# Narrow fp32 products cut into pieces of 64 columns, step sizes as four-strip products, a carried state read by halves of its rows

## The chip, the cores and the metric

The program runs on one core of one Trainium2 chip. What counts is the device time of one execution in microseconds (us). A core has TensorE (PE, matrix products, with PEld for its weight loads), VectorE (DVE), ScalarE (ACT), GpSimd (POOL), SyncE (SP, which here issues every transfer) and 16 DMA engines. TensorE's clock has two levels, 2.4 and 1.2 GHz; the profile gives the granted share.

## The reference, cut to what matters

One inference step of a hybrid decoder: 16 meta tokens and 1024 prompt tokens, and 8 sequences that decode one token each. There are 2 layers, D = 1024, and three groups of heads run side by side in a layer.

```python
for l in range(2):
    h = rmsnorm(x)
    q, k, v, u, z, xBC, dt = split(h @ W_in)      # dt: 4 columns, one for each SSD head
    A = rmsnorm(sliding_window_attention(q, k, v))   # 8 heads, window 128, sinks
    B = rmsnorm(glu(gelu(s5_scan(u))))               # diagonal state space
    # SSD: xs, B, C from a causal convolution of xBC; step = softplus(dt + bias)
    # chunks of 128 tokens: y = (C B^T * decay) (step * xs) + C (carried state) * decay + D * xs
    C = rmsnorm(ssd(xs, B, C, step) * silu(z))
    x = x + concat(A, B, C) @ W_out
    x = x + swiglu(rmsnorm(x))
y = rmsnorm(x)
```

## The kernel before, in words

Features lie on the partitions, tokens along the free dimension. The 1048 tokens are cut into two halves (528 and 520 columns), each half into two chunks (264 and 264, or 264 and 256; in the last layer's output stages 256 and 256). The unit of program is (layer, half).

The large projections are done by `mm3` (lines 206 to 213): weights and activations are split into a rounded part and a rest, and each tile of 128 x 128 weights makes three float32r products with 264 or 256 moving columns. I call these the wide products: L211, L212 and L213, 16,896 instructions of TensorE's 20,006. Among them the code weaves the small products of the mixers, which are plain fp32. An fp32 product shows in the trace as two MATMUL records, each with its weight load; a float32r product, a bf16 product and a transpose (against `ident`, L614, L971, L1252 and others) show as one.

The lines that the change touches:

- `rstd_diag` (239): the sum of squares over the partitions, as products of pieces of `acc` against a column of ones, one moving column each (L245). A chunk of 264 gives three products with 88 weight columns, one of 256 two with 128, a block of attention one with 128. Its result goes through ACT, DVE, another product (L258, or L1171 in attention) to the engine that scales by it.
- `in_proj` (321) with `weights_dt` (189): one of its 15 steps computes `dt`, 16 products for each chunk against a tile that is 4 columns wide in substance and padded to 128 (L339, L340); the sum is scaled on DVE and stored as 4 rows.
- `s5_prep` (371): taps of the S5 convolution, 128 weight columns against 32 moving ones, two products summed (L624).
- `ssd` (841): reads `dt`, turns it to tokens on partitions (L899, L904), sums the decays with `tri` and `ones` (L929, L943), then for each chunk of 128 tokens the products L1016 (inside the chunk), L1019 (with the state `hT` carried into the chunk) and L1024 (the new state). For L1019 the C matrix was padded with zeros to 128 rows in two copies `Cz`, one for each group:

```python
V.tensor_mul(cz4[:, 1], cz4[:, 0], Cz[1][:, cols].unsqueeze(1).to_broadcast([128, 2, nq]))
V.tensor_mul(cz4[:, 0], cz4[:, 0], Cz[0][:, cols].unsqueeze(1).to_broadcast([128, 2, nq]))
```

- `attn_dec` (1305): the decode step's scores and values, 128 weight columns of a cache against 8 moving ones for each of 8 sequences (L1326, L1361).

The order on every engine is set when the program is built, by a scheduler that follows an estimated timeline and priorities; on the chip TensorE then takes its products in that order. Accumulators are six banks `x` (`pmx`, three for the tag `o`, three for `a`) and two banks `b` (`pbig`).

Of the kernel before, what the change touches and what calls it, by code (L numbers as in the profile page):

```python
# [31 lines left out]
EPS = 1e-6  # L32
MT = 'u0 u1 k v q0 q1 q2 q3 xs0 xs1 B C dt z0 z1'.split()


def build(ctx, tc, A):
# [87 lines left out]
    evn = [0]  # L124

    def evac(out, in_):
        evn[0] += 1
        if evn[0] % 2:
            S.copy(out, in_)
        else:  # L130
            V.tensor_copy(out, in_)
# [56 lines left out]

    def weights_dt(l, mi):

        raw = wp.tile([128, 8, 128], F32, tag="wr", name=nm("wr"), bufs=2)
        with tc.high_priority(offset=3000):
            load(raw, A["w_in"][l, mi])
        wh = wp.tile([128, 8, 128], F32R, tag="wh", name=nm("wh"))
        S.copy(wh, raw)
        wl = wp.tile([128, 8, 128], F32R, tag="wl", name=nm("wl"))
        S.copy(wl, raw)
        V.tensor_sub(wl[:, :, 32:36], raw[:, :, 0:4], wh[:, :, 0:4].bitcast(F32))
        return wh, wl

    def split(dst, cols, src, eng=None):
# [37 lines left out]
    def rstd_diag(acc, n, scale):  # L239

        nb = -(-n // 128)
        w = n // nb
        ps = pmx()
        for j in range(nb):
            PE.matmul(ps[0:w, 504 + j:505 + j], acc[:, j * w:j * w + w], ones[:, 0:1], start=True, stop=True)  # L245
        sm = small()[0:w, 0:nb]
        S.activation(sm, ps[0:w, 504:504 + nb], AF.Sqrt, bias=epst[0:w, 0:1], scale=scale)
        V.reciprocal(sm, sm)
        dg = ftp.tile([128, 264], F32, tag="dg", name=nm("dg"))
        V.tensor_mul(dg[0:w, :n].rearrange("p (j q) -> p j q", j=nb), ident[0:w, 0:w].unsqueeze(1).to_broadcast([w, nb, w]),  # L250
                     sm.unsqueeze(2).to_broadcast([w, nb, w]))
        return w, dg
# [38 lines left out]
    for l in range(DEPTH):  # L291
        for hf in range(2):
            T = TH[hf]
            for n_ in ("xs0", "xs1", "B", "C", "k", "v", "z0", "z1"):
                P[l, hf, n_] = dram([128, T], n_)
            P[l, hf, "dt"] = dram([4, T], "dt")
            P[l, hf, "u"] = dram([2, 128, 8 * NK8[hf]], "u")
# [8 lines left out]
    def in_norm(l, hf, new):  # L306
# [4 lines left out]
        for c0, c1 in CH[hf]:  # L311
            acc = None
            for k, t in enumerate(x[hf]):
# [3 lines left out]
                acc = add_square(acc, t[:, c0:c1], c1 - c0)  # L317
            rstd_sum(acc, c1 - c0, 1.0 / D, rs[:, c0:c1])
        return xn, rs

    def in_proj(l, hf, xr, early=0):
# [5 lines left out]
        for mi, name in enumerate(MT):  # L327
            w = weights(A["w_in"][l, mi], 8) if name != "dt" else weights_dt(l, mi)
            st = stp.tile([128, 528], F32, tag="st", name=nm("st"))
            for c0, c1 in CH[hf]:  # L330
# [4 lines left out]
                else:  # L335
                    ps = pbig()
                if name == "dt":
                    for k in range(8):
                        PE.matmul(ps[:, :n], w[1][:, k, :], xn[k][:, 0, c0:c1], start=(k == 0), stop=False)  # L339
                        PE.matmul(ps[:, :n], w[0][:, k, :], xn[k][:, 1, c0:c1], start=False, stop=(k == 7))  # L340
                    S.copy(st[0:4, c0:c1], ps[32:36, :n])
                    V.tensor_add(st[0:4, c0:c1], st[0:4, c0:c1], ps[0:4, :n])
                    V.tensor_mul(st[0:4, c0:c1], st[0:4, c0:c1], rs[0:4, c0:c1])
                    continue
                mm3(ps[:, :n], w, xn, c0, c1)
# [9 lines left out]
            with tc.high_priority(offset=3000):  # L355
                if name == "dt":
                    load(P[l, hf, "dt"], st[0:4, :T])
                elif name[0] == "u":
                    load(P[l, hf, "u"][int(name[1])], st[:, :8 * nk])
# [11 lines left out]
    def s5_prep(l):  # L371
# [199 lines left out]
        for p in range(0, 8, 2):  # L571
# [49 lines left out]
            for a in range(2):  # L621
                g = 2 * (p + a) % 8
                for e in range(2):
                    PE.matmul(pk_[:, 16 * g:16 * g + 32], w_[e][:, 144 * a:144 * a + 128],  # L624
                              bz[:, 256 * e + 32 * (p + a):256 * e + 32 * (p + a) + 32], start=(e == 0), stop=(e == 1))
            if p % 4 == 2:
# [214 lines left out]
    def ssd(l, hf):  # L841
# [50 lines left out]
        dr = slot()  # L892
        load(dr[0:4, :T], P[l, hf, "dt"])
        sm5 = kvp.tile([128, 9, 20], F32, tag="ssds", name=nm("ssds"), bufs=2)
# [3 lines left out]
        for i in range(4):  # L898
            PE.transpose(pt[:, 4 * i:4 * i + 4], dr[0:4, f0 + 128 * i:f0 + 128 * i + 128], ident[0:4, 0:4])  # L899
        V.tensor_copy(v_[:, 0:16], pt[:, 0:16])  # L900
        pt2 = pmx()
        ne = 16 if hf == 0 else 8
        o5 = 0 if hf == 0 else NP
        PE.transpose(pt2[0:ne, 0:4], dr[0:4, o5:o5 + ne], ident[0:4, 0:4])  # L904
        V.tensor_copy(v_[0:ne, 16:20], pt2[0:ne, 0:4])
# [22 lines left out]
        pc = pmx()  # L928
        PE.matmul(pc[:, 0:n5], tri, dA[:, 0:n5], start=True, stop=True)  # L929
        V.tensor_copy(cs[:, 0:n5], pc[:, 0:n5])  # L930
# [11 lines left out]
        pl = pmx()  # L942
        PE.matmul(pl[:, 0:16], ones, dA[:, 0:16], start=True, stop=True)  # L943
        if hf == 0:
# [17 lines left out]
        for c0, nq, bi in blocks:  # L962
# [37 lines left out]
            if hT is not None:  # L1000
# [6 lines left out]
                ce = slot()  # L1007
                cz4 = ce[:, 0:4 * nq].rearrange("p (g r i) -> p g r i", g=2, r=2)
                S.activation(ce[:, 0:2 * nq], pce[:, 0:2 * nq], AF.Exp)
                V.tensor_mul(cz4[:, 1], cz4[:, 0], Cz[1][:, cols].unsqueeze(1).to_broadcast([128, 2, nq]))  # L1010
                V.tensor_mul(cz4[:, 0], cz4[:, 0], Cz[0][:, cols].unsqueeze(1).to_broadcast([128, 2, nq]))
            for t in range(2):
                py = pmx()
                for r in range(2):
                    o_ = py[64 * r:64 * r + 64, 0:nq]
                    PE.matmul(o_, xd_[0:nq, (2 * t + r) * 64:(2 * t + r) * 64 + 64],  # L1016
                              E[0:nq, (2 * t + r) * nq:(2 * t + r + 1) * nq], start=True, stop=(hT is None))
                    if hT is not None:
                        PE.matmul(o_, hT[:, r, :], cz4[:, t, r, :], start=False, stop=True)  # L1019
                V.scalar_tensor_tensor(yt[t][:, cols], X[t][:, cols], par("ssdd", l)[:, t:t + 1], py[:, 0:nq],  # L1020
                                       ALU.mult, ALU.add)
# [283 lines left out]
    def attn_dec(l, cos, sin, kn, vt, oT):  # L1305
# [16 lines left out]
        for hb in range(2):  # L1322
            kc = slot()
            load(kc[:, 0:512].rearrange("p (b k) -> p b k", b=4), A["ckt"][l, :, 4 * hb:4 * hb + 4, :])
            for b in range(4):
                PE.matmul(ps[:, (4 * hb + b) * 8:(4 * hb + b) * 8 + 8], kc[:, b * 128:b * 128 + 128],  # L1326
                          qz[:, (4 * hb + b) * 8:(4 * hb + b) * 8 + 8], start=True, stop=True)
        st_ = small()
# [28 lines left out]
        for hb in range(2):  # L1357
            vc = slot()
            load(vc[:, 0:512].rearrange("p (b k) -> p b k", b=4), A["cv"][l, 4 * hb:4 * hb + 4].rearrange("b k d -> k b d"))
            for b in range(4):  # L1360
                PE.matmul(p5[:, (4 * hb + b) * 8:(4 * hb + b) * 8 + 8], vc[:, b * 128:b * 128 + 128],  # L1361
                          pT[:, (4 * hb + b) * 8:(4 * hb + b) * 8 + 8], start=True, stop=True)
        on = small()
# [226 lines left out]
def _host(i):  # L1590
# [16 lines left out]

    wcols["dt"] = np.concatenate([wcols["dt"], np.zeros((2, 1024, 124), f)], axis=2)

# [128 lines left out]
```

## Time and profile before

| what | value |
|---|---|
| three runs | 2468.42, 2474.44, 2476.19 us; median 2474.44 |
| profiled execution | 2467.74 us; its span from first to last instruction 2465.9 us |
| TensorE busy with products, with weight loads | 97%, 94% of the span |
| VectorE, ScalarE, GpSimd busy | 59%, 43%, 14% |
| mean granted TensorE clock | 0.986 of full speed |
| transfers | 298.92 MB, mean 121 GB/s |

Busy times of TensorE overlap, since its products are pipelined: a wide product lasts 0.28 us but the next starts 0.12 us after it. What a product costs is read from start to start of its neighbours.

### The profile page before, as it was taken

How to read it: one execution, taken by the hardware profiler on the slowest of the kernel's cores; microseconds unless marked ns; L12 is line 12 of the kernel's file. 1: busy time of each engine (PE TensorE's matmuls, PEld its weight loads, DVE VectorE, ACT ScalarE, POOL GpSimd, SP SyncE). 2: the span in 40 equal slices, each digit the busy share in tenths (PEclk: the TensorE clock that was granted, in tenths of full speed). 3: DMA queues.
4: the chain of work that ended last, by engine and by line, in shares of the span. 5: the costliest groups of instructions: out<-in, count | busy, mean ns of one | idle time of the engine just before them, and what ended most of it. 6: DMA issues, size and time to landing. Idle time of an engine off the chain costs nothing.

```text
span 2465.9 us, 49857 instructions
## 1 busy us (share of the span) xinstructions
PE 2390.1 (97%) x20006; PEld 2310.0 (94%) x20006; DVE 1462.5 (59%) x3502; ACT 1050.1 (43%) x2157; POOL 348.3 (14%) x476
## 2 busy tenths in 40 slices
PE   8999789999999999999999999999999999999998
PEld 7889689999999999999899999999999999999997
DVE  8777667656558655564664545665565447434344
ACT  5465544334553533343553443343454435323224
POOL 6302130011003220001110021000110004000000
PEclk9999899999999999999999999999999999999998
DMA  7555232544324534253432324346432233322322
GB/s 248 184 171 158 86 98 75 152 142 156 90 82 144 180 113 144 71 167 95 140 93 86 108 95 142 124 137 181 139 105 85 85 117 120 96 86 95 95 84 80
DMA packets 201558, 298.92 MB, mean 121 GB/s; under 512 B 55776, under 2 KB 132400, under 8 KB 201296
## 3 DMA queue, kind: packets, MB, share of 16 engines
q1 hardware_dynamic: 201328, 295.74, 38.5%
q8 instruction: 157, 2.57, 0.4%
q14 instruction: 73, 0.60, 0.1%
HBM read 254.78 MB, written 45.09 MB: 122 GB/s over the span
## 4 chain that ended last, share of the span: by engine, by line
PE 83%; DVE 8%; DMA 4%; ACT 3%; issue 2%; SPq 1%; POOL 0%; DVEq 0%; ACTq 0%; POOLq 0%
PE pb L211 24%; PE pb L212 24%; PE pb L213 23%; DVE wl L186 1%; PE px L1268 1%; PE px L1223 1%; SPq L121 1%; PE px L258 1%; ACT wh L184 1%; PE px L1271 1%; PE px L1252 1%; PE px L817 1%; PE px L212 1%; DMA hs<-dq 1%; PE px L213 1%
## 5 line engine op out<-in xcount | busy, mean ns | idle before, releaser
L211 PE MATMUL pb<-hh,wh 128*128 128x264 f32 (+1 forms) x3200 | 917.1, 287 | 17.0 <-DVE th L1448 14.5
L212 PE MATMUL pb<-hh,wh 128*128 128x264 f32 (+1 forms) x3200 | 914.3, 286 | 2.4 <-DVE hh L204 2.4
L213 PE MATMUL pb<-hh,wl 128*128 128x264 f32 (+1 forms) x3200 | 910.9, 285 | 0.0
L211 PE MATMUL pb<-hl,wh 128*128 128x264 f32 (+1 forms) x2304 | 661.8, 288 | 13.6 <-DVE st L350 4.0
L212 PE MATMUL pb<-hl,wh 128*128 128x264 f32 (+1 forms) x2304 | 659.6, 286 | 0.6 <-DVE hl L316 0.5
L213 PE MATMUL pb<-hl,wl 128*128 128x264 f32 (+1 forms) x2304 | 658.0, 286 | 0.0
L184 ACT CAST wh<-wr 128x512 fp32r<-128x512 f32 (+2 forms) x536 | 386.9, 753 | 599.4 <-PE pb L212 537.8
L211 PEld LDWEIGHTS pb<-hh,wh 128*128 128x128 f32 x3200 | 606.1, 189 | 25.4 <-DVE th L1448 18.1
L212 PEld LDWEIGHTS pb<-hh,wh 128*128 128x128 f32 x3200 | 604.9, 189 | 5.8 <-DVE hh L204 2.5
L213 PEld LDWEIGHTS pb<-hh,wl 128*128 128x128 f32 x3200 | 606.2, 189 | 4.2 <-issue 3.3
L186 DVE TENSOR_TENSOR wl<-wr,wh 128x512 fp32r<-128x512 f32 (+2 forms) x536 | 465.6, 890 | 177.9 <-ACT wh L184 170.7
L211 PEld LDWEIGHTS pb<-hl,wh 128*128 128x128 f32 x2304 | 437.5, 190 | 21.5 <-issue 10.6
L212 PEld LDWEIGHTS pb<-hl,wh 128*128 128x128 f32 x2304 | 436.8, 190 | 3.7 <-issue 1.7
L213 PEld LDWEIGHTS pb<-hl,wl 128*128 128x128 f32 x2304 | 437.2, 190 | 1.8 <-issue 1.5
L228 POOL TENSOR_TENSOR sq<-sq,sq 128x264 f32<-128x264 f32 (+1 forms) x142 | 119.1, 844 | 687.0 <-ACT sq L225 600.7
L1464 DVE TENSOR_TENSOR x<-x,pb 128x264 f32<-128x264 f32 (+1 forms) x176 | 74.3, 423 | 142.9 <-PE pb L213 141.8
L1449 DVE SCALAR_TENSOR_TENSOR th<-th,pb 128x264 f32<-128x264 f32 (+1 forms) x176 | 74.6, 424 | 139.7 <-PE pb L213 139.1
L203 ACT CAST hl<-th 128x264 fp32r<-128x264 f32 (+1 forms) x176 | 71.7, 408 | 194.9 <-DVE th L1449 194.5
L1448 DVE SCALAR_TENSOR_TENSOR th<-th,pb 128x264 f32<-128x264 f32 (+1 forms) x176 | 74.2, 421 | 77.5 <-ACT th L1447 77.2
L1447 ACT ACTIVATE th<-pb 128x264 f32<-128x264 f32 (+1 forms) x176 | 67.7, 384 | 102.7 <-PE pb L213 102.2
L225 ACT ACTIVATE sq<-x 128x264 f32<-128x264 f32 (+1 forms) x160 | 64.0, 416 | 103.5 <-DVE x L1428 60.3
L204 DVE TENSOR_TENSOR hl<-th,hl 128x264 fp32r<-128x264 f32 (+1 forms) x176 | 83.8, 476 | 28.1 <-ACT hl L203 27.3
(426 smaller groups left out, 2572.2 us busy)
## 6 DMA issues: line engine op xcount, KB each, us to landing
wr<-w_gate SPq DMA_DIRECT2D x88, 512.0 KB, 3.2
wr<-w_up SPq DMA_DIRECT2D x88, 512.0 KB, 3.3
wr<-w_down SPq DMA_DIRECT2D x64, 512.0 KB, 3.5
wr<-w_in SPq DMA_DIRECT2D x60, 512.0 KB, 3.2
wr<-w_out SPq DMA_DIRECT2D x32, 512.0 KB, 3.2
wr<-w_down SPq DMA_DIRECT2D x32, 384.0 KB, 3.1
x<-xt SPq DMA_DIRECT2D x48, 132.0 KB, 4.0
s<-ds5v SPq DMA_DIRECT2D x16, 256.0 KB, 3.0
```

The source lines that it names most:

```text
L184: S.copy(wh[:, a:b], raw[:, a:b])
L186: V.tensor_sub(wl[:, a:b], raw[:, a:b], wh[:, a:b].bitcast(F32))
L203: S.copy(h, src)
L204: (eng or V).tensor_sub(l, src, h.bitcast(F32))
L211: PE.matmul(ps, wh[:, k, :], ah, start=(k == order[0]), stop=False)
L212: PE.matmul(ps, wh[:, k, :], al, start=False, stop=False)
L213: PE.matmul(ps, wl[:, k, :], ah, start=False, stop=(k == order[-1]))
L228: (eng or G).tensor_tensor(acc[:, :n], acc[:, :n], sq[:, :n], ALU.add)
L1447: S.activation(th[:, :n], pg[:, :n], AF.Tanh, scale=0.5)
L1448: V.scalar_tensor_tensor(th[:, :n], th[:, :n], 1.0, pg[:, :n], ALU.add, ALU.mult)
L1449: V.scalar_tensor_tensor(th[:, :n], th[:, :n], 0.5, pu[:, :n], ALU.mult, ALU.mult)
L1464: V.tensor_add(x[hf][m][:, c0:c1], x[hf][m][:, c0:c1], ps[:, :n])
```

## The change

A helper `halves` sends out a product with more than 64 weight columns as pieces of at most 64, each writing its own rows of the same accumulator; a product of 88 becomes one of 64 and one of 24. It is used for L245, L624, L929, L943, L1326, L1361 and for what were the transposes L899. The step `dt` is gone from `in_proj`. In its place `in_dt` multiplies x itself (not split, the gain folded into the weights) in fp32: the eight tiles of features go out as two rounds of four products with 32 weight columns, each on a strip of 32 rows of the accumulator; the 4 x 4 partial rows are stored as 16 and added up where `ssd` turns them to tokens. For (0,1) it is called at the end of `in_norm`, else before the third step of `in_proj`. The product with the carried state now takes only the 64 rows of its group, and stands behind the four of the chunk.

```diff
@@ -123,6 +123,13 @@
+    def halves(o_, lhsT, rhs, start=True, stop=True):
+
+        M = lhsT.shape[-1]
+        for m in range(0, M, 64):
+            e = min(m + 64, M)
+            PE.matmul(o_[m:e], lhsT[:, m:e], rhs, start=start, stop=stop)
+
     def evac(out, in_):
...
@@ -186,18 +193,6 @@
-    def weights_dt(l, mi):
-
-        raw = wp.tile([128, 8, 128], F32, tag="wr", name=nm("wr"), bufs=2)
-        with tc.high_priority(offset=3000):
-            load(raw, A["w_in"][l, mi])
-        wh = wp.tile([128, 8, 128], F32R, tag="wh", name=nm("wh"))
-        S.copy(wh, raw)
-        wl = wp.tile([128, 8, 128], F32R, tag="wl", name=nm("wl"))
-        S.copy(wl, raw)
-        V.tensor_sub(wl[:, :, 32:36], raw[:, :, 0:4], wh[:, :, 0:4].bitcast(F32))
-        return wh, wl
-
     def split(dst, cols, src, eng=None):
...
@@ -242,7 +237,7 @@
         for j in range(nb):
-            PE.matmul(ps[0:w, 504 + j:505 + j], acc[:, j * w:j * w + w], ones[:, 0:1], start=True, stop=True)
+            halves(ps[0:w, 504 + j:505 + j], acc[:, j * w:j * w + w], ones[:, 0:1])
         sm = small()[0:w, 0:nb]
...
@@ -316,7 +311,27 @@
             rstd_sum(acc, c1 - c0, 1.0 / D, rs[:, c0:c1])
+        if (l, hf) == (0, 1):
+            in_dt(l, hf, rs)
         return xn, rs
+
+    def in_dt(l, hf, rs):
+        g = par("ln1", l)
+
+
+        wdt = slot()[:, 0:256].rearrange("p (k m) -> p k m", k=8)
+        load(wdt, A["w_dt"][l])
+        V.tensor_mul(wdt, wdt, g.unsqueeze(2).to_broadcast([128, 8, 32]))
+        st = stp.tile([128, 528], F32, tag="st", name=nm("st"))
+        for c0, c1 in CH[hf]:
+            ps = pmx()
+            for q in range(2):
+                for j in range(4):
+                    PE.matmul(ps[32 * j:32 * j + 32, :c1 - c0], wdt[:, 4 * q + j, :], x[hf][4 * q + j][:, c0:c1],
+                              start=(q == 0), stop=(q == 1))
+            V.tensor_mul(st[:, c0:c1], ps[:, :c1 - c0], rs[:, c0:c1])
+        for j in range(4):
+            load(P[l, hf, "dt"][4 * j:4 * j + 4], st[32 * j:32 * j + 4, :TH[hf]])
...
@@ -325,7 +340,9 @@
         for mi, name in enumerate(MT):
-            w = weights(A["w_in"][l, mi], 8) if name != "dt" else weights_dt(l, mi)
+            if mi == 2 and (l, hf) != (0, 1):
+                in_dt(l, hf, rs)
+            w = weights(A["w_in"][l, mi], 8)
             st = stp.tile([128, 528], F32, tag="st", name=nm("st"))
...
@@ -334,14 +351,6 @@
                     ps = pbig()
-                if name == "dt":
-                    for k in range(8):
-                        PE.matmul(ps[:, :n], w[1][:, k, :], xn[k][:, 0, c0:c1], start=(k == 0), stop=False)
-                        PE.matmul(ps[:, :n], w[0][:, k, :], xn[k][:, 1, c0:c1], start=False, stop=(k == 7))
-                    S.copy(st[0:4, c0:c1], ps[32:36, :n])
-                    V.tensor_add(st[0:4, c0:c1], st[0:4, c0:c1], ps[0:4, :n])
-                    V.tensor_mul(st[0:4, c0:c1], st[0:4, c0:c1], rs[0:4, c0:c1])
-                    continue
                 mm3(ps[:, :n], w, xn, c0, c1)
...
@@ -621,8 +628,8 @@
                 for e in range(2):
-                    PE.matmul(pk_[:, 16 * g:16 * g + 32], w_[e][:, 144 * a:144 * a + 128],
-                              bz[:, 256 * e + 32 * (p + a):256 * e + 32 * (p + a) + 32], start=(e == 0), stop=(e == 1))
+                    halves(pk_[:, 16 * g:16 * g + 32], w_[e][:, 144 * a:144 * a + 128],
+                           bz[:, 256 * e + 32 * (p + a):256 * e + 32 * (p + a) + 32], e == 0, e == 1)
             if p % 4 == 2:
...
@@ -890,18 +897,20 @@
         dr = slot()
-        load(dr[0:4, :T], P[l, hf, "dt"])
+        load(dr[0:16, :T], P[l, hf, "dt"])
+        s16 = small()
+        V.tensor_reduce(s16[0:16, 0:4], ident[0:16, 0:16].rearrange("p (j h) -> p h j", h=4), axis=AX.X, op=ALU.add)
         sm5 = kvp.tile([128, 9, 20], F32, tag="ssds", name=nm("ssds"), bufs=2)
...
         for i in range(4):
-            PE.transpose(pt[:, 4 * i:4 * i + 4], dr[0:4, f0 + 128 * i:f0 + 128 * i + 128], ident[0:4, 0:4])
+            halves(pt[:, 4 * i:4 * i + 4], dr[0:16, f0 + 128 * i:f0 + 128 * i + 128], s16[0:16, 0:4])
         V.tensor_copy(v_[:, 0:16], pt[:, 0:16])
...
         o5 = 0 if hf == 0 else NP
-        PE.transpose(pt2[0:ne, 0:4], dr[0:4, o5:o5 + ne], ident[0:4, 0:4])
+        PE.matmul(pt2[0:ne, 0:4], dr[0:16, o5:o5 + ne], s16[0:16, 0:4], start=True, stop=True)
         V.tensor_copy(v_[0:ne, 16:20], pt2[0:ne, 0:4])
...
@@ -926,7 +935,7 @@
         pc = pmx()
-        PE.matmul(pc[:, 0:n5], tri, dA[:, 0:n5], start=True, stop=True)
+        halves(pc[:, 0:n5], tri, dA[:, 0:n5])
         V.tensor_copy(cs[:, 0:n5], pc[:, 0:n5])
...
@@ -1005,19 +1014,20 @@
                 ce = slot()
-                cz4 = ce[:, 0:4 * nq].rearrange("p (g r i) -> p g r i", g=2, r=2)
+                c3 = ce[:, 0:2 * nq].rearrange("p (r i) -> p r i", r=2)
                 S.activation(ce[:, 0:2 * nq], pce[:, 0:2 * nq], AF.Exp)
-                V.tensor_mul(cz4[:, 1], cz4[:, 0], Cz[1][:, cols].unsqueeze(1).to_broadcast([128, 2, nq]))
-                V.tensor_mul(cz4[:, 0], cz4[:, 0], Cz[0][:, cols].unsqueeze(1).to_broadcast([128, 2, nq]))
+                V.tensor_mul(c3, c3, Ct[:, cols].unsqueeze(1).to_broadcast([128, 2, nq]))
+            py = [pmx(), pmx()]
+            for h in range(4):
+                PE.matmul(py[h // 2][64 * (h % 2):64 * (h % 2) + 64, 0:nq], xd_[0:nq, h * 64:h * 64 + 64],
+                          E[0:nq, h * nq:(h + 1) * nq], start=True, stop=(hT is None))
+            if hT is not None:
+                for r in range(2):
+                    for t in range(2):
+                        gp = slice(64 * t, 64 * t + 64)
+                        PE.matmul(py[t][64 * r:64 * r + 64, 0:nq], hT[gp, r, :], c3[gp, r, :], start=False, stop=True)
             for t in range(2):
-                py = pmx()
-                for r in range(2):
-                    o_ = py[64 * r:64 * r + 64, 0:nq]
-                    PE.matmul(o_, xd_[0:nq, (2 * t + r) * 64:(2 * t + r) * 64 + 64],
-                              E[0:nq, (2 * t + r) * nq:(2 * t + r + 1) * nq], start=True, stop=(hT is None))
-                    if hT is not None:
-                        PE.matmul(o_, hT[:, r, :], cz4[:, t, r, :], start=False, stop=True)
-                V.scalar_tensor_tensor(yt[t][:, cols], X[t][:, cols], par("ssdd", l)[:, t:t + 1], py[:, 0:nq],
+                V.scalar_tensor_tensor(yt[t][:, cols], X[t][:, cols], par("ssdd", l)[:, t:t + 1], py[t][:, 0:nq],
                                        ALU.mult, ALU.add)
...
@@ -1323,8 +1333,8 @@
             for b in range(4):
-                PE.matmul(ps[:, (4 * hb + b) * 8:(4 * hb + b) * 8 + 8], kc[:, b * 128:b * 128 + 128],
-                          qz[:, (4 * hb + b) * 8:(4 * hb + b) * 8 + 8], start=True, stop=True)
+                halves(ps[:, (4 * hb + b) * 8:(4 * hb + b) * 8 + 8], kc[:, b * 128:b * 128 + 128],
+                       qz[:, (4 * hb + b) * 8:(4 * hb + b) * 8 + 8])
         st_ = small()
...
@@ -1605,7 +1615,8 @@
-    wcols["dt"] = np.concatenate([wcols["dt"], np.zeros((2, 1024, 124), f)], axis=2)
+    wdt = i["w_in"][:, :, cols["dt"]].reshape(2, 8, 128, 4).transpose(0, 2, 1, 3)
+    r["w_dt"] = c(np.concatenate([wdt, np.zeros((2, 128, 8, 28), f)], axis=3).astype(f))
```

What stands on TensorE, as lines of each program's order (line, operation, out<-in, shape of the moving operand's result; xN counts equal neighbours). First a sum of squares of a chunk of 264 in the first layer, second half, with the wide products around it. Before:

```order
L213 MATMUL pb_6138<-hh_4425,wl_6045 128x264
L245 MATMUL px_5564<-cones_95,sq_5559 88x1 x3
L211 MATMUL pb_6240<-hl_4597,wh_6236 128x264
L212 MATMUL pb_6240<-hl_4597,wh_6236 128x264
L213 MATMUL pb_6240<-hl_4597,wl_6237 128x264
```

After (L206 to L208 are the wide products there, L131 the helper):

```order
L208 MATMUL pb_6158<-hh_4430,wl_6065 128x264
L131 MATMUL px_5579<-cones_95,sq_5574 64x1
L131 MATMUL px_5579<-cones_95,sq_5574 24x1
L131 MATMUL px_5579<-cones_95,sq_5574 64x1
L131 MATMUL px_5579<-cones_95,sq_5574 24x1
L131 MATMUL px_5579<-cones_95,sq_5574 64x1
L131 MATMUL px_5579<-cones_95,sq_5574 24x1
L206 MATMUL pb_6260<-hl_4608,wh_6256 128x264
```

Three products of one width became six whose width alternates. Of the 23 such chains of three, 21 stand like this in the order after; two are broken up by wide products.

Second, the step sizes of the second layer's first half: before, 16 products for each chunk among the wide ones of `in_proj`.

```order
L339 MATMUL pb_11870<-hl_11031,wl_11866 128x264
L340 MATMUL pb_11870<-hl_11031,wh_11864 128x264
L339 MATMUL pb_11870<-hl_11032,wl_11866 128x264
L340 MATMUL pb_11870<-hl_11032,wh_11864 128x264
L339 MATMUL pb_11870<-hl_11033,wl_11866 128x264
L340 MATMUL pb_11870<-hl_11033,wh_11864 128x264
```

After, 8 products for each chunk, at another place; here a sum of squares has come between the two chunks' products:

```order
L330 MATMUL px_11333<-x_3941,s_11329 32x264
L330 MATMUL px_11333<-x_3942,s_11329 32x264
L330 MATMUL px_11343<-x_3935,s_11329 32x264
L131 MATMUL px_12108<-cones_95,sq_12085 64x1
L131 MATMUL px_12108<-cones_95,sq_12085 24x1
L131 MATMUL px_12108<-cones_95,sq_12085 64x1
L131 MATMUL px_12108<-cones_95,sq_12085 24x1
L131 MATMUL px_12108<-cones_95,sq_12085 64x1
L131 MATMUL px_12108<-cones_95,sq_12085 24x1
L330 MATMUL px_11343<-x_3936,s_11329 32x264
L330 MATMUL px_11343<-x_3937,s_11329 32x264
```

The step has moved from the middle of `in_proj` to its beginning, and the x tiles are its moving operand.

Third, a chunk of the SSD with a carried state. Before:

```order
L1016 MATMUL px_2748<-s_2732,s_2718 64x128
L1019 MATMUL px_2748<-s_2744,hT_2644 64x128
L1016 MATMUL px_2748<-s_2732,s_2718 64x128
L1019 MATMUL px_2748<-s_2744,hT_2644 64x128
L1016 MATMUL px_2754<-s_2732,s_2718 64x128
L1019 MATMUL px_2754<-s_2744,hT_2644 64x128
L1016 MATMUL px_2754<-s_2732,s_2718 64x128
L1019 MATMUL px_2754<-s_2744,hT_2644 64x128
L1024 MATMUL px_2760<-s_2718,s_2721 64x128 x2
```

After:

```order
L1022 MATMUL px_2790<-s_2775,s_2761 64x128 x2
L1022 MATMUL px_2791<-s_2775,s_2761 64x128 x2
L1028 MATMUL px_2790<-s_2787,hT_2686 64x128
L1028 MATMUL px_2791<-s_2787,hT_2686 64x128
L1028 MATMUL px_2790<-s_2787,hT_2686 64x128
L1028 MATMUL px_2791<-s_2787,hT_2686 64x128
L1034 MATMUL px_2802<-s_2761,s_2764 64x128 x2
```

The four products with the state (64 rows each now) stand together between the other two kinds (128 rows).

## Rows read from the trace of the kernel before

**Rows 1.** The page: span, and part 1, busy time by engine.
```profile
span 2465.9 us, 49857 instructions
PE 2390.1 (97%) x20006; PEld 2310.0 (94%) x20006; DVE 1462.5 (59%) x3502; ACT 1050.1 (43%) x2157; POOL 348.3 (14%) x476
```
**Rows 2.** Waits of TensorE: total us, times, longest; first and last of 26.
```profile
PE pb L211 <- DVE th L1448: 14.5, 12, 3.2
...
PE px L985 <- DVE s L1020: 0.2, 1, 0.2
```
**Rows 3.** One stretch by engine: busy us (count), then PEclk, DMA share, GB/s.
```profile
2100.00:2400.00 300.00, 300.00 (x2509) 300.00 (x2508) 123.15 (x230) 83.37 (x161) 0.00 (x0) 1.00 0.29 92
```
**Rows 4.** Timeline of PE: start us, us to the last end, operation, count of records.
```profile
889.71 0.28 PE L212 MATMUL pb<-hl,wh 128*128 128x264 f32 x1
889.83 0.28 PE L213 MATMUL pb<-hl,wl 128*128 128x264 f32 x1
889.95 0.56 PE L245 MATMUL px<-cones,sq 128*88 128x1 f32 x6
890.37 0.37 PE L211 MATMUL pb<-hl,wh 128*128 128x264 f32 x1
890.58 0.28 PE L212 MATMUL pb<-hl,wh 128*128 128x264 f32 x1
```
**Rows 5.** The same view at an S5 tap (128 columns).
```profile
771.22 0.28 PE L212 MATMUL pb<-hh,wh 128*128 128x264 f32 x1
771.34 0.75 PE L624 MATMUL px<-s,s 128*128 128x32 f32 x6
...
772.13 0.29 PE L211 MATMUL pb<-hh,wh 128*128 128x264 f32 x1
```
**Rows 6.** The same view at two pieces of 64 columns.
```profile
1004.24 0.28 PE L211 MATMUL pb<-hh,wh 128*128 128x264 f32 x1
1004.46 0.29 PE L956 MATMUL px<-ssds,cones 128*64 128x8 f32 x4
1004.67 0.39 PE L212 MATMUL pb<-hh,wh 128*128 128x264 f32 x1
1004.90 0.28 PE L213 MATMUL pb<-hh,wl 128*128 128x264 f32 x1
```
**Rows 7.** The same view where width goes from 64 to 16 columns.
```profile
501.85 0.29 PE L761 MATMUL px<-chz,s 128*64 128x64 f32 x4
501.97 0.29 PE L765 MATMUL px<-ut,s 128*64 128x64 f32 x4
502.19 0.23 PE L778 MATMUL px<-csz,s 128*16 128x8 f32 x2
502.27 0.21 PE L779 MATMUL px<-ut,s 128*16 128x8 f32 x2
502.34 0.21 PE L778 MATMUL px<-csz,s 128*16 128x8 f32 x2
```
**Rows 8.** Groups by line and shape: count | busy us, mean ns | idle before.
```profile
L245 PE MATMUL px<-cones,sq 128*88 128x1 f32 x138 | 13.9, 212 | 0.7 <-POOL sq L228 0.6
L340 PE MATMUL pb<-hl,wh 128*128 128x264 f32 x48 | 13.6, 312 | 0.0
```
**Rows 9.** Timeline of PE at one fp32 product of 264 moving columns.
```profile
1138.71 0.28 PE L213 MATMUL pb<-hl,wl 128*128 128x256 f32 x1
1138.83 0.61 PE L817 MATMUL px<-s,s 128*128 128x264 f32 x2
...
1139.40 0.28 PE L212 MATMUL pb<-hl,wh 128*128 128x264 f32 x1
```
**Rows 10.** Timeline of PE where two attention products start side by side.
```profile
703.01 0.43 PE L1268 MATMUL px<-s,s 128*64 128x256 f32 x1
703.02 0.43 PE L1271 MATMUL px<-s,s 128*64 128x256 f32 x1
```
**Rows 11.** Two stretches by engine, as in Rows 3, after L1361 in layer 0.
```profile
589.20:592.60 3.40, 3.40 (x29) 3.19 (x28) 1.80 (x6) 0.60 (x3) 0.00 (x0) 1.00 0.44 134
592.60:596.00 3.40, 3.40 (x18) 3.40 (x17) 1.89 (x3) 2.09 (x4) 1.83 (x3) 0.51 0.65 175
```

More of the change, by code (lines that the diff above doesn't have):

```diff
@@ L32 @@
 EPS = 1e-6
-MT = 'u0 u1 k v q0 q1 q2 q3 xs0 xs1 B C dt z0 z1'.split()
+MT = 'u0 u1 k v q0 q1 q2 q3 xs0 xs1 B C z0 z1'.split()
 def build(ctx, tc, A):
@@ L295, in build @@
                 P[l, hf, n_] = dram([128, T], n_)
-            P[l, hf, "dt"] = dram([4, T], "dt")
+            P[l, hf, "dt"] = dram([16, T], "dt")
             P[l, hf, "u"] = dram([2, 128, 8 * NK8[hf]], "u")
@@ L355, in in_proj @@
             with tc.high_priority(offset=3000):
-                if name == "dt":
-                    load(P[l, hf, "dt"], st[0:4, :T])
-                elif name[0] == "u":
+                if name[0] == "u":
                     load(P[l, hf, "u"][int(name[1])], st[:, :8 * nk])
@@ L942, in ssd @@
         pl = pmx()
-        PE.matmul(pl[:, 0:16], ones, dA[:, 0:16], start=True, stop=True)
+        halves(pl[:, 0:16], ones, dA[:, 0:16])
         if hf == 0:
@@ L1360, in attn_dec @@
             for b in range(4):
-                PE.matmul(p5[:, (4 * hb + b) * 8:(4 * hb + b) * 8 + 8], vc[:, b * 128:b * 128 + 128],
-                          pT[:, (4 * hb + b) * 8:(4 * hb + b) * 8 + 8], start=True, stop=True)
+                halves(p5[:, (4 * hb + b) * 8:(4 * hb + b) * 8 + 8], vc[:, b * 128:b * 128 + 128],
+                       pT[:, (4 * hb + b) * 8:(4 * hb + b) * 8 + 8])
         on = small()
```

## The prediction

> **What bounds the kernel now.** I read the page's first part first: TensorE is busy for 97% of the span, VectorE for 59%, ScalarE for 43% [rows 1]. Busy time of pipelined products proves little, so next come TensorE's waits: 26 kinds, 67 us in all, the largest 14.5 us [rows 2]. So some 2400 of 2466 us are TensorE's own queue, and over the last long stretch it has no gap at all (300 us of 300) [rows 3]. Products leave in the order in which they are queued, and each delays all behind it. What a change of the small products is worth is therefore read from the timeline, from the start of the wide product ahead to the start of the second wide product behind, less two steps of 0.12 us (that from one wide product to the next) [rows 4].
>
> **Prices.** An uncut chain of three products of 88 columns takes 0.75 us from 889.83 to 890.58, less 0.24: 0.51, or 0.17 each [rows 4]. Three of 128 columns take 0.91 less 0.24: 0.67, or 0.22 each [rows 5]. The kernel already has products in pieces of 64. One lone pair, two halves side by side, takes 0.66 less 0.24: 0.42 [rows 6]. Inside a run of such pairs one more pair takes 0.12 (501.85 to 501.97) [rows 7]. So a run of pairs costs 0.30 to open and close, and 0.12 for each pair: a lone pair loses 0.20 against an uncut product of 128, two pairs lose 0.10, three are even, long runs win 0.10 a pair.
>
> Where the opening goes can be seen: the first piece starts 0.22 after the last wide product instead of 0.12, and the second wide product behind comes 0.23 after the first instead of 0.12 [rows 6]; the rest lies between the pieces' last start and the first wide one. It is paid at a change of width between narrow products, too: four records of 64 columns had just taken 0.12 us, but the first of 16 columns starts 0.22 after them, and its two records take 0.08 instead of the 0.07 of those behind it [rows 7]. So a change inside a narrow run costs 0.10.
>
> **The change part by part.** All in TensorE time, by the order of both programs.
>
> - Step sizes, removed: 128 wide products of 0.12 (48 of them in one group of [rows 8]): -15.5 us.
> - Step sizes, added: 8 chunks of two rounds of four strips, two records each. One fp32 product of 264 columns takes 0.69 less 0.24, 0.45 for two records, so 0.22 each [rows 9]. The trace shows two products on different columns starting 0.01 us apart [rows 10]; four strips at once it does not show. If they run abreast, 8 x 4 x 0.22 = 7.0 us, and with some seven openings of 0.30 (the order parts two of the four calls) 9.1. If two run abreast, 7 more, and one after the other 21 more. I take 9.1, since the row is of the same mechanism.
> - The 23 chains of three products of 88 (138 records [rows 8]): each is now 64, 24, 64, 24, 64, 24. The piece of 64 costs 0.21 until the next width may start (1004.46 to 1004.67) [rows 6], the piece of 24, by the nearest row, that of 16 columns, 0.08 and 0.10 for the change [rows 7]. Three times 0.39 is 1.17; 0.10 to enter and 0.11 behind make 1.38, against 0.51: +0.87 a chain, 20 us for 23. Some chains adjoin other narrow work and share an opening: I take +19. The lower bound is that 64 and 24 go side by side like two halves: 0.30 + 3 x 0.12 = 0.66, +0.15 a chain, +3.5 in all.
> - Sums of squares with 128 columns: 16 alone (+0.20 each) and 13 chains of two (+0.10): +4.5.
> - S5 taps: 32 products in 12 runs: 12 x 0.30 - 32 x 0.10 = +0.4.
> - Decode scores and values: 32 products in 5 runs: 1.5 - 3.2 = -1.7.
> - Turning the step sizes and summing the decays, four units of three short runs: from nothing to an opening each less a little, 0 to +2.4; I take +1.
> - Carried state, 16 chunks: four products abreast instead of two and two saves one round of 128 columns, 0.22 by half of the price of 264 [rows 9], and adds one or two changes with a new set of rows, 0.10 to 0.15 each [rows 6, 7]: nothing to +0.1 a chunk. I take +0.8.
>
> Sum: -15.5 + 9.1 + 19 + 4.5 + 0.4 - 1.7 + 1 + 0.8 = +17.6 us.
>
> What else moves: ScalarE and VectorE lose the split of the padded weights, VectorE one of two multiplications in each chunk, the transfers 2 MB of 299. Neither engine is the bound [rows 1], and all that TensorE waits for anything is 67 us [rows 2]; I give it nothing, and up to 5 us in the range. The four transfers that store the 16 rows, on SP's queue, are issued early in `in_proj`, long before `ssd` reads them. The longer chains stand ahead of the products that bring the norm back, but TensorE does not stand still for it: the delay is the queue's and counted already. In `in_norm` and at the end, where it waits, it comes on top all the same, since the wait starts at the chain's end.
>
> The clock is the last unknown. After the sixteen records of L1361 the granted clock falls from 1.00 to 0.51, that is to 1.2 GHz, for 3.4 us, in which 18 records start, where 29 did before [rows 11]; such a stretch costs 1.7 us. The narrow chains grow longer, the decode's run shorter. Three stretches more or fewer are 5 us; I take none.
>
> One rule of the Trainium skill speaks against this change. TensorEngine Tiling, section "Key Properties", says that changing the tiling mode, not just the tile, drains the engine; the trace agrees, with its 0.10 us at a change from 64 to 16 columns. By that rule the piece of 24 drains the engine on both sides, as in my sum; without it the chain would cost its lower bound.
>
> **The rivals.**
>
> 1. Widths share. The pieces of 64 and 24 run side by side without a change. The chains then cost 3.5 instead of 19: the sum falls to +2, 2476 us. For it: they write different rows and use different columns. Against it: [rows 7], where a narrower piece waits although it is only the width that is new.
> 2. Strips queue. The strips do not run four abreast: two abreast +24.6, one at a time +38.6, 2499 and 2513 us. For it: four moving operands are read at once, which nothing here does. Against it: [rows 10].
>    TensorE: Matmul & The Clock Gate of the Trainium skill, part 3, has 2.38 times for three strips; by an estimate from that, four would lose about 2 us more than my 9.1, which no run here shows yet.
> 3. Faster: the changes of width hide under the wide products' weight loads and products queued behind. Then only steady prices are left: -15.5 + 7.0 for the step sizes, the chains 69 x (0.12 - 0.17) = -3.5, sums of 128 42 x -0.10 = -4.2, taps and decode 64 x -0.10 = -6.4: -22.6, so 2452 us. Counted along the orders, the products change between full and narrow width or between narrow kinds 606 times after and 310 times before; so it decides at 22.6 / 296 = 0.076 us a change. Below it the change is faster. The lone pair pays 0.30 for two changes, 0.15 each [rows 6], the one inside a run 0.10 [rows 7]. For it: only that hundreds of openings may sit next to waits, where they are free.
>
> **How the numbers follow.** The profiled execution took 2467.7 us, 6.7 below the median of the runs; its sum gives 2485.3, and the same 17.6 on the median 2474.4 gives 2492. I give the forecast 0.64, the first rival 0.13, the second 0.09, the third 0.14. Less than 0.3%, 7.4 us, is about what a measurement of this kernel can't tell from no change. The likeliest case alone, with 5 us each for clock and waits and the runs' spread of 8 us, covers 2480 to 2502. The range over all cases reaches from 2464, with the first rival inside, its 5 us for waits and clock too, to 2513, the second rival's worse end; about 0.14 below it is left out. Slower by over 0.3%: the forecast nearly whole (0.59), the second rival (0.09) and a little of the first (0.02), 0.70. Same: the forecast's low edge (0.05) and most of the first rival (0.09), 0.14. Faster: the third, and the first with a gain at the waits, 0.16.
>
> **What would show it.** In the timeline after, a chain of three sums of 88 should take 1.3 to 1.4 us between wide products where 0.51 stood; if 0.7, the first rival holds. The strips should start within 0.02 us of each other in fours, a chunk's eight products taking near 1 us; 2 or 4 us is the second. A lone pair should cost 0.42, the decode runs should shrink by 0.4 to 0.6 us each. TensorE's waits should stay near 67 us. The forecast is wrong if the span grows by less than 8 us while those chains measure 1.4, for then the openings lie where TensorE would have waited.

## The result: 18 us slower, as forecast in sum, for two causes where I had named one

The changed kernel takes 2490.61 us in the median of 4 runs (2487.21 to 2493.65), the kernel before 2472.15 us in the same comparison: a ratio of 1.0076 (95% interval 1.006 to 1.0091), some 18.5 us slower. The forecast was 2492 in a range of 2464 to 2513. The page of the changed kernel, where [rows 1] stood, and then its largest waits, where [rows 2] stood:

```profile
span 2491.9 us, 50649 instructions
PE 2399.8 (96%) x20424; PEld 2294.3 (92%) x20424; DVE 1454.3 (58%) x3482; ACT 1037.0 (42%) x2139; POOL 347.9 (14%) x476
```
```profile
PE pb L206 <- DVE th L1458: 13.8, 15, 2.9
PE px L330 <- DVE s L324: 11.3, 1, 11.3
PE px L253 <- DVE dg L245: 10.5, 6, 3.9
PE px L206 <- ACT hl L310: 7.4, 1, 7.4
```

TensorE's busy time went from 2390.1 to 2399.8 us, 9.7 more where the forecast had 17.6. Its idle time (span less busy) went from 75.8 to 92.1 us, 16.3 more where the forecast had nothing. All TensorE waits together, which should have stayed near 67 us, add up to 84 (79 in a second profile, e8). One line of the waits is new: the first strips stand for 11.3 us until their weights are multiplied by the gain.

The timeline of a chain of three sums of 88, now six pieces in twelve records (start us, us to the last end, operation, count), which answers to [rows 4]:

```profile
1088.49 0.28 PE L207 MATMUL pb<-hh,wh 128*128 128x256 f32 x1
1088.69 1.10 PE L131 MATMUL px<-cones,sq 128*64 128x1 f32 x12
1089.73 0.39 PE L208 MATMUL pb<-hh,wl 128*128 128x256 f32 x1
1089.95 0.28 PE L206 MATMUL pb<-hh,wh 128*128 128x256 f32 x1
```

From 1088.49 to 1089.95 less two steps of 0.12 is 1.22 us, where 0.51 stood. (The name of the row, 128*64, is that of its first piece.) Eight chains that stand alone among wide products, with no wait, take 1.23 us each, within 0.01.

### The profile page after: what moved, and what is told of

Its sections match the earlier page's. It is cut to its first block, busy times and chain, and to the rows that moved or that the text cites. A ratio compares the mean times of both kernels' runs of the same rounds, so it can differ in the third digit from the quotient of the medians.

```text
span 2491.9 us, 50649 instructions
## 1 busy us (share of the span) xinstructions
PE 2399.8 (96%) x20424; PEld 2294.3 (92%) x20424; DVE 1454.3 (58%) x3482; ACT 1037.0 (42%) x2139; POOL 347.9 (14%) x476
## 5 line engine op out<-in xcount | busy, mean ns | idle before, releaser
L206 PE MATMUL pb<-hh,wh 128*128 128x264 f32 (+1 forms) x3200 | 915.9, 286 | 14.9 <-DVE th L1458 13.0
L208 PE MATMUL pb<-hh,wl 128*128 128x264 f32 (+1 forms) x3200 | 910.6, 285 | 0.0
L206 PE MATMUL pb<-hl,wh 128*128 128x264 f32 (+1 forms) x2304 | 661.6, 288 | 15.4 <-DVE x L1474 5.2
L208 PE MATMUL pb<-hl,wl 128*128 128x264 f32 (+1 forms) x2304 | 655.8, 285 | 0.0
L206 PEld LDWEIGHTS pb<-hh,wh 128*128 128x128 f32 x3200 | 605.2, 189 | 23.9 <-DVE th L1458 17.2
L208 PEld LDWEIGHTS pb<-hh,wl 128*128 128x128 f32 x3200 | 605.3, 189 | 4.3 <-issue 3.3
L193 DVE TENSOR_TENSOR wl<-wr,wh 128x512 fp32r<-128x512 f32 (+2 forms) x536 | 465.2, 890 | 183.9 <-ACT wh L191 177.8
L206 PEld LDWEIGHTS pb<-hl,wh 128*128 128x128 f32 x2304 | 436.1, 189 | 25.8 <-issue 6.5
L208 PEld LDWEIGHTS pb<-hl,wl 128*128 128x128 f32 x2304 | 435.5, 189 | 2.7 <-issue 2.5
L1458 DVE SCALAR_TENSOR_TENSOR th<-th,pb 128x264 f32<-128x264 f32 (+1 forms) x176 | 73.9, 420 | 75.8 <-ACT th L1457 75.6
```

The costliest lines, as they stand in the source:

```text
L193: V.tensor_sub(wl[:, a:b], raw[:, a:b], wh[:, a:b].bitcast(F32))
L206: PE.matmul(ps, wh[:, k, :], ah, start=(k == order[0]), stop=False)
L208: PE.matmul(ps, wl[:, k, :], ah, start=False, stop=(k == order[-1]))
L1458: V.scalar_tensor_tensor(th[:, :n], th[:, :n], 1.0, pg[:, :n], ALU.add, ALU.mult)
```

## The two causes in the trace

The new wait reads backwards. These rows are, in turn, from the timelines of SyncE's issues, of VectorE and of TensorE in the changed kernel:

```profile
38.90 0.38 SPq L121 DMA_DIRECT2D ut<-du  x1
47.01 2.37 SPq L121 DMA_DIRECT2D wr<-w_in  x2
49.44 0.42 SPq L121 DMA_DIRECT2D s<-w_dt  x1
```
```profile
45.77 1.22 DVE L193 TENSOR_TENSOR wl<-wr,wh 128x1024 fp32r<-128x1024 f32 x1
...
47.82 1.21 DVE L193 TENSOR_TENSOR wl<-wr,wh 128x1024 fp32r<-128x1024 f32 x1
...
54.31 0.42 DVE L324 TENSOR_TENSOR s<-s,cpack 128x256 f32<-128x256 f32 x1 [1.25 <-DMA s<-w_dt]
```
```profile
43.19 0.28 PE L208 MATMUL pb<-hl,wl 128*128 128x264 f32 x1
54.79 3.30 PE L330 MATMUL px<-x,s 128*32 128x264 f32 x32 [11.32 <-DVE s L324]
```

VectorE is in the middle of the S5 preparation and splits the weights of two steps late (L193, ending at 46.99 and 49.03). Two weight loads wait on SyncE's queue for the buffers that this frees. The 128 KB for the step sizes stand behind them and are issued at 49.44, VectorE multiplies them at 54.31, and TensorE, which ran out at 43.5, has them next in its order. The wide products behind them don't pass, though they are ready sooner: in e5 below, where the strips are queued behind them, TensorE doesn't wait here.

The clock is low, too. In the middle of the wait the granted clock falls to half, that is to 1.2 GHz, and it stays there over most of the strips (busy us of each engine, TensorE's products and weight loads first; then PEclk, DMA share, GB/s):

```profile
47.30:57.40 10.10, 2.61 (x24) 1.17 (x28) 8.37 (x42) 0.00 (x0) 4.03 (x12) 0.50 0.90 258
```

The first 100 us of the kernel before, and then the stretches of the first 420 us of the changed kernel, in the same view:

```profile
0.00:100.00 100.00, 85.55 (x645) 83.70 (x646) 84.12 (x245) 48.52 (x89) 55.72 (x78) 0.95 0.70 223
```

```profile
0.00:100.00 100.00, 77.25 (x626) 72.77 (x626) 82.50 (x238) 44.51 (x85) 53.00 (x75) 0.93 0.66 206
100.00:250.00 150.00, 138.13 (x1283) 124.50 (x1279) 114.54 (x333) 80.39 (x183) 29.72 (x40) 0.98 0.54 163
250.00:420.00 170.00, 149.59 (x1144) 136.59 (x1144) 107.36 (x259) 81.04 (x179) 31.67 (x37) 0.90 0.31 95
```

The strips themselves do what I took from [rows 9, 10]. Here in the second layer sixteen records, a chunk's eight products, take 1.02 us until the next narrow product starts: four abreast, whose starts lie within 0.02 us, and the next four 0.22 us behind them:

```profile
1515.76 0.28 PE L208 MATMUL pb<-hl,wl 128*128 128x256 f32 x1
1515.97 1.09 PE L330 MATMUL px<-x,s 128*32 128x264 f32 x16
1516.99 0.40 PE L131 MATMUL px<-cones,sq 128*64 128x1 f32 x8
```

## The experiments

Ratios are to the kernel before, timed beside it on the same chip, with 95% intervals. The kernel before took 2474.44 us in the median beside e1 to e4, 2471.98 beside e5 to e8, and 2468.33 in one run beside e9 and e10, so differences of medians are good to a few us only. Busy, idle and clock are TensorE's in the profiled execution, which can lie 5 or 6 us from its kernel's median (e4 2463.93, e7 2461.51).

| kernel | median us | ratio | busy | idle | clock |
|---|---|---|---|---|---|
| before | 2472.15 | 1 | 2390.1 | 75.8 | 0.986 |
| before, profiled again (e9) | 2468.49 (1 run) | | 2388.4 | 78.2 | 0.987 |
| changed | 2490.61 | 1.0076 (1.006 to 1.0091) | 2399.8 | 92.1 | 0.984 |
| changed, profiled again (e8) | 2488.65 (1 run) | | 2399.9 | 87.0 | 0.985 |
| e1, sums of 88 uncut | 2474.92 | 1.0004 (0.9992 to 1.0015) | 2377.8 | 90.1 | 0.988 |
| e2, second piece of 64 | 2476.33 | 1.0007 (0.9995 to 1.0019) | 2386.7 | 85.6 | 0.986 |
| e3, pieces sorted by width | 2484.06 | 1.0038 (1.0023 to 1.0053) | 2393.8 | 90.3 | 0.983 |
| e4, first weights early | 2469.88 | 0.9979 (0.9968 to 0.9991) | 2392.5 | 69.6 | 0.988 |
| e5, first strips later | 2473.45 | 1.0011 (1.0001 to 1.0021) | 2395.7 | 74.8 | 0.988 |
| e6, no strips | 2480.64 | 1.0036 (1.0022 to 1.005) | 2400.1 | 78.4 | 0.987 |
| e7, e4 with sums uncut | 2456.3 | 0.994 (0.9927 to 0.9952) | 2379.8 | 79.9 | 0.986 |
| e10, nothing halved | 2478.63 (1 run) | | 2387.4 | 89.3 | 0.983 |

My theory was that each change of width between narrow pieces costs, and that the queue passes it on; the rival, once the new wait was seen, that the wait costs all and the chains nothing.

**e1, the sums of 88 uncut.** In `halves`:

```diff
-        for m in range(0, M, 64):
-            e = min(m + 64, M)
+        w = 64 if M % 64 == 0 else M
+        for m in range(0, M, w):
+            e = m + w
```

> The changed kernel, but products of 88 weight columns go out uncut again; those of 128 stay in halves. Theory (each change of width between narrow pieces costs TensorE about 0.1 us, and the queue passes it on to the end): a chain of three takes 0.50 to 0.55 us between wide products where the changed kernel shows 1.23, so 23 x 0.7 = 16 us come back, near 2474 us. Rival (the chains are covered, what costs is the new wait at the first strips): the chain falls to 0.5 just the same, but the time stays within 4 us of 2490.

A chain takes 0.50 us again (1073.03 to 1073.77 less 0.24) and 15.7 us come back in the median, though the strips still wait 7.8 us. The theory holds against this rival; what in the longer chain costs is for the next two to tell.

```profile
1073.03 0.28 PE L208 MATMUL pb<-hh,wh 128*128 128x256 f32 x1
1073.15 0.56 PE L132 MATMUL px<-cones,sq 128*88 128x1 f32 x6
1073.56 0.36 PE L209 MATMUL pb<-hh,wl 128*128 128x256 f32 x1
1073.77 0.28 PE L207 MATMUL pb<-hh,wh 128*128 128x256 f32 x1
```

**e2 and e3, as many pieces with fewer changes of width.** In `rstd_diag`, for e2 and for e3:

```diff
         for j in range(nb):
-            halves(ps[0:w, 504 + j:505 + j], acc[:, j * w:j * w + w], ones[:, 0:1])
+            if w == 88 and j < 2:
+                halves(ps[0:128, 504 + j:505 + j], acc[:, j * w:j * w + 128], ones[:, 0:1])
+            else:
+                halves(ps[0:w, 504 + j:505 + j], acc[:, j * w:j * w + w], ones[:, 0:1])
```
```diff
-        for j in range(nb):
-            halves(ps[0:w, 504 + j:505 + j], acc[:, j * w:j * w + w], ones[:, 0:1])
+        for m in range(0, w, 64):
+            e = min(m + 64, w)
+            for j in range(nb):
+                PE.matmul(ps[m:e, 504 + j:505 + j], acc[:, j * w + m:j * w + e], ones[:, 0:1], start=True, stop=True)
```

> The changed kernel, but in a chain of three the first two products send a second piece of 64 columns instead of 24 (its last 40 columns run on into the next product's and land in rows that nobody reads); the third keeps 64 and 24. The chain then changes its width once inside instead of five times, with as many pieces and more columns. Theory (the change costs): the chain takes 0.75 to 0.82 us instead of 1.23, 23 x 0.45 = 10 us less, near 2480 us. Rival (the number of pieces costs): the chain stays at 1.2 us, the time at 2490.

> The changed kernel, but a chain of three sends its three pieces of 64 first, then its three of 24: the same six pieces, one change of width inside instead of five. The pieces of 64 then stand on the same columns of the array and can't run side by side. Theory (the change costs): 0.85 to 0.95 us a chain instead of 1.23, 23 x 0.33 = 7.5 us less, near 2483 us. Rival (the pieces cost): 1.2 us a chain, 2490.

The timelines of one chain, of e2 and of e3:

```profile
1075.18 0.28 PE L207 MATMUL pb<-hh,wh 128*128 128x256 f32 x1
1075.39 0.65 PE L131 MATMUL px<-cones,sq 128*64 128x1 f32 x12
1075.96 0.38 PE L208 MATMUL pb<-hh,wl 128*128 128x256 f32 x1
1076.19 0.28 PE L206 MATMUL pb<-hh,wh 128*128 128x256 f32 x1
```
```profile
1080.36 0.28 PE L207 MATMUL pb<-hh,wh 128*128 128x256 f32 x1
1080.57 0.75 PE L242 MATMUL px<-cones,sq 128*64 128x1 f32 x12
1081.25 0.38 PE L208 MATMUL pb<-hh,wl 128*128 128x256 f32 x1
1081.47 0.28 PE L206 MATMUL pb<-hh,wh 128*128 128x256 f32 x1
```

0.77 and 0.87 us, as expected, with twelve records each like the 1.22. e3 has the very same pieces, four changes fewer and 0.35 us less: 0.09 us a change, and that without two pieces running side by side (in e3 the records of 64 columns start 0.06 us apart, in e2 the two of a pair 0.01). So it is the change of width that costs, not the number of pieces. By the Trainium skill (TensorEngine Tiling, section "Key Properties") a change of the tiling mode drains the engine; the 0.09 us agree with it. In time e3 gained 6.5 us (expected 7.5) and e2 14.3 (expected 10), more than its chains explain (23 x 0.45 = 10). Against the changed kernel's profile e2's has 13.1 us less busy and 6.5 less idle time, and idle time alone differs by 5 us between two profiles of the changed kernel, so where the rest lies is not shown.

**e4 and e5, the first strips freed from their wait.** e4 takes a slot, loads the weights and multiplies them at the start of `in_norm`, ahead of the constants, and `in_dt` then takes them from there (of its edit, the part in `in_norm`); e5 only calls later:

```diff
         rs = slot()
+        if (l, hf) == (0, 0):
+            wd00.append(slot()[:, 0:256].rearrange("p (k m) -> p k m", k=8))
+            load(wd00[0], A["w_dt"][l])
+            V.tensor_mul(wd00[0], wd00[0], g.unsqueeze(2).to_broadcast([128, 8, 32]))
```
```diff
-            if mi == 2 and (l, hf) != (0, 1):
+            if mi == (6 if (l, hf) == (0, 0) else 2) and (l, hf) != (0, 1):
```

> The changed kernel, but the first step sizes' weights are loaded and multiplied by the gain at the start of the norm, before the constants, instead of behind two weight loads that wait for their buffers. The strips then stand some 65 products earlier on TensorE. If the 11.3 us wait of the first strips is the new work's own: TensorE's waits in the first 100 us fall by about 8 us and the time by as much, near 2482 us. If the wide products behind it would have waited for their weights anyway: the wait moves to them or to the next of the start's waits, and the time stays within 3 us of 2490.

> The changed kernel, but for the first half of the first layer the step sizes' products are called before the seventh step of the input projection instead of the third; their weights are loaded as late as before. The strips then stand 100 products later on TensorE, some 12 us of ready work. Theory (the first strips wait for their weights with ready products queued behind them): the 11.3 us wait shrinks to under 3 and the time falls by 10 to 20 us, towards the 2470 us of the early load. Rival (the early load gained by another order of the whole start): the time stays within 5 us of 2490.

Both took the wait away and both gained more than it: 20.7 and 17.2 us in the median (24 and 16 by the ratios). For e4 my 8 us were much too few. In e4 the transfer goes out at 13.9 us; in e5 it goes out at 51.2, later than in the changed kernel, and still TensorE doesn't wait for it. In both the 32 records run at full clock; the transfer and the strips of e4, then the strips of e5:

```profile
13.88 0.33 SPq L121 DMA_DIRECT2D s<-w_dt  x1
```
```profile
31.44 0.61 PE L253 MATMUL px<-dg,cones 88*128 88x264 f32 x2
31.98 1.99 PE L339 MATMUL px<-x,s 128*32 128x264 f32 x32
```
```profile
56.51 1.99 PE L330 MATMUL px<-x,s 128*32 128x264 f32 x32
```

The stretches of e4 show in which part of the run the rest lies:

```profile
0.00:100.00 100.00, 86.43 (x711) 81.73 (x712) 86.17 (x245) 46.71 (x87) 57.37 (x80) 0.98 0.73 228
100.00:250.00 150.00, 145.18 (x1337) 128.62 (x1336) 117.29 (x358) 91.36 (x212) 26.86 (x39) 0.97 0.54 159
250.00:420.00 170.00, 152.39 (x1199) 140.38 (x1198) 107.98 (x258) 80.50 (x174) 28.47 (x34) 0.92 0.31 92
```

Against the changed kernel TensorE is idle 9.2 us less in the first 100, 7.0 less in the next 150 and 2.8 less in the 170 after: the later waits are shorter too. That a late start delays VectorE and the loads behind it, and that the later waits grow by this, is my reading; no run takes it apart. The granted clock of the first 100 us is 0.98 instead of 0.93, worth up to 5 us by an estimate (0.05 of 100 us). That e5, with another place for the strips and the load as late as before, gains nearly as much speaks against luck of one order. And with the wait gone the change as a whole is nearly level with the kernel before: 0.2% faster in e4, 0.1% slower in e5.

**e6, the step sizes as before, all else changed.** `weights_dt`, the `dt` step and the transposes of the 4 rows are those of the kernel before.

> The changed kernel without its new step sizes: they are again one step of the input projection with padded weights, as in the kernel before; all other parts of the change stay. Theory (the strips save TensorE 15.5 - 11.5 = 4 us of work and cost 20 us by their first wait): 2490 + 4 - 20 = 2474 us, 4 us above the version with the early load. Rival (the early load's gain was luck of the order): 2494 us.

1.0036, some 10 us under the changed kernel, where 16 were expected: nearer to the theory than to the rival, but the halves and the carried state alone cost only 9 us of time against the kernel before, not the 24 that my terms for them add up to. Against e4 the strips, once they don't wait, are worth some 11 to 14 us, more than the 6.4 that I gave them; in the profiles 7.6 us of that are busy time, near my term, and the rest is idle time.

**e7, early weights and uncut sums.** e4 with L245 as it was before the change.

> The changed kernel with the early load of the first step sizes' weights and with the sums of squares uncut, of 88 and of 128 columns; the decode, the S5 taps and the products in the state space part stay in halves. If the two causes add up: 2490 - 20.7 (early load) - 15.7 (88 uncut) - 4 (128 uncut) = 2450 us, faster than both kernels. Rival (the uncut sums only fill the waits that the early load has emptied): 2466 to 2470 us.

2456.3 us, a ratio of 0.994: about 15 us faster than the kernel before and 34 faster than the changed one. The two causes don't add up in full: uncutting gains 13.6 us here in the median (9.6 by the ratios) where 20 were expected. In the profiles busy time falls by 12.7, the clock is 0.986 instead of 0.988, and idle time grows by 10.3 us. Whether those are waits that the longer chains had filled is not shown: these two profiled executions lie only 2.4 us apart, where the medians lie 13.6.

**e8 to e10, repeats and nothing halved.** In e10 `halves` sends every product whole.

> The changed kernel as it is, profiled a second time. TensorE's idle time, 92.1 us in the first profile, within 5 us of it; the first strips wait 8 to 12 us again.

> The kernel before as it is, profiled a second time, to see how far its TensorE times repeat: busy 2390 us within 2, idle 76 us within 5.

> The changed kernel with every product of more than 64 columns uncut again; the strips with their late weights and the carried state's four products stay. By the forecast's terms TensorE's busy time falls by 19 + 4.5 + 0.4 - 1.7 + 1 = 23 us against the changed kernel's 2399.8; if the sums of 128 and the other halves cost less than forecast and only the chains count, by 15 to 17 us. TensorE's idle time stays near 90 us, since the first strips wait as before.

Busy and idle time repeat within 2 and 5 us; the strips waited 8.3 us in the second profile of the changed kernel, 11.1 in e10. All halves together are 12.4 us of busy time, less than either number expected. In time, e10's one run is 10.3 us above the one run of the kernel before beside it: so the late strips and the carried state cost about that without any halves, as far as one run of each tells.

## Why the prediction was right, point by point, and what was luck

- **The chains of 88: right mechanism, a little smaller.** 0.72 us more a chain instead of 0.87; 23 make 16.6 instead of 19, and e1 got 15.7 back. The chain's 1.22 us lies a little under the 1.3 to 1.4 that I had named as the sign. The first rival (widths share, 0.66 us a chain) is refuted by the timeline: 1.22. The third needed changes under 0.076 us; e3 measures 0.09, which is close: by that rival's own count 296 changes at 0.09 make the change 4 us slower, not 17.6.
- **Openings and sums of 128: right.** A lone pair costs 0.41 (748.39 to 749.04 less 0.24; forecast 0.42 [rows 6]), so +0.2 against 0.22 uncut. In the timelines the sums of an attention block, with the products beside them, go from 0.70 to 0.88 us and the chains of two from 0.45 to 0.53.

```profile
748.39 0.28 PE L208 MATMUL pb<-hh,wl 128*128 128x264 f32 x1
748.60 0.28 PE L131 MATMUL px<-cones,s 128*64 128x1 f32 x4
748.82 0.39 PE L206 MATMUL pb<-hh,wh 128*128 128x264 f32 x1
749.04 0.28 PE L207 MATMUL pb<-hh,wh 128*128 128x264 f32 x1
```

- **The decode: right sign, larger.** A run of 8 products, now 16 pieces in 32 records, takes 1.26 us (592.06 to 593.56 less 0.24) where it took 1.79 (575.40 to 577.43 less 0.24): 0.5 less, as forecast; the two runs of values save 0.75 each. All five save 2.5 us, forecast 1.7. The run before and after:

```profile
575.40 0.28 PE L213 MATMUL pb<-hh,wl 128*128 128x264 f32 x1
575.52 1.85 PE L1326 MATMUL px<-m,s 128*128 128x8 f32 x16
577.22 0.37 PE L211 MATMUL pb<-hh,wh 128*128 128x264 f32 x1
577.43 0.28 PE L212 MATMUL pb<-hh,wh 128*128 128x264 f32 x1
```
```profile
592.06 0.28 PE L207 MATMUL pb<-hh,wh 128*128 128x264 f32 x1
592.27 1.13 PE L131 MATMUL px<-m,s 128*64 128x8 f32 x32
593.33 0.39 PE L208 MATMUL pb<-hh,wl 128*128 128x264 f32 x1
593.56 0.28 PE L206 MATMUL pb<-hh,wh 128*128 128x264 f32 x1
```

- **The carried state: wrong sign, small.** I had +0.8 us. In the two units without a wait among these products (second half, both layers) the four chunks' products take 6.35 us each time, where they took 6.98 and 7.14: some 0.2 us less a chunk, by an estimate from these eight 3 us less over sixteen.
- **The strips' price: right; the second rival, that they queue, is refuted.** What failed is the step "I give it nothing, and up to 5 us in the range". Of `in_dt`'s transfers I had traced the four stores, and not the load and the multiplication ahead of its products, though SyncE's and VectorE's queues both stand in the way. That wait and what follows it cost 17 to 21 us (e4, e5), more than the 5 that I allowed, and the sign that I had named, TensorE's waits near 67 us, did not come true: they are 84.
- **The clock: "I take none" was nearly right.** (1 - clock) x span is 34.5 and 32.1 us in the two profiles of before, 39.9 and 37.3 in those of the changed kernel: an estimate of 5 us more, within the 5 that I allowed. In the first 100 us it goes with the wait: 0.93 in the changed kernel, e8, e1, e2 and e10 and 0.95 in e3, all with it, but 0.98 in e4 to e7, without it (the kernel before has 0.95 and 0.98). Over the whole span it does not: 29.6 us in e1, with the wait, and 34.4 in e7, without.
- **The sum was right by luck.** Terms of 17.6 us of work became about 10 (9.7 and, in the repeats, 11.5 us of busy time, in which the slower clock's 5 are counted), and the waits that I had left out added 9 to 16. By time, the 24 us of the halves and the carried state became 9 (e6), the 6.4 that the strips save became 11 to 14, and the wait that I had at nothing cost 17 to 21. With the wait gone the change is nearly level with the kernel before (e4, e5), and so it is with the wait left and the chains uncut (e1). So the chains were one of two causes, and taking either away takes away the whole difference. Without the wait, which I had left out, the change would have come out between 5 us faster (e4) and 3 us slower (e5). Size and direction were saved by an omission.

What stays open: the chains and the halves that I can read one by one add up to some 18 us or more (16.6, less 2.5 for the decode, and 4 for the sums of 128: 16 by 0.18 and 13 by 0.08), yet busy time shows 12.4 between the changed kernel and e10, and 10 to 12 between e6 and before, where the carried state's 3 are saved as well. Busy time counts the stretches at the lower clock at their full length. With (1 - clock) x span taken off it, an estimate, the first difference is 15 to 17 us, near the 18, and the second some 12, where 15 were to be expected. The 3 us left I can't place.

## What to carry to other kernels

In this kernel, cutting a narrow fp32 product into pieces paid only in long runs of pieces of one width (the decode); a piece of another width in between cost a change each way. Of the 0.72 us that a chain lost, sorting by width gave back 0.35 and padding to the common width 0.45; leaving the chain uncut gave back all. When a product moves, follow every input back to its DMA issue: a small transfer that queues behind loads which wait for buffers can cost more than all the work that the move saves. And a total that comes out right is no proof of its terms: compare busy and idle time apart, and take out each cause by itself.

## What I had not expected of the hardware

Four column strips at once run with no loss that the trace shows: a chunk's sixteen records take 1.02 us, four times the 0.22 of one record [rows 9] and what it costs to leave the strips' width, as if each four were one. TensorE: Matmul & The Clock Gate of the Trainium skill, part 3, has 2.38 times for three strips. Here four, of another length (264 moving columns, fp32), are near four times.

The first wait cost twice: after its 11.3 us the strips run mostly at a granted clock of 0.50, 32 records in 3.30 us to their last end, where e4 and e5 take 1.99 for them with no wait ahead.
